# Attention's weights times values in plain fp32 with the turned weights stationary, and the sums of the second MLP product on VectorE

## The chip, the cores and the metric

One Trainium2 chip; the program uses one of its NeuronCores. A core has TensorE (PE, with its weight loads PEld), VectorE (DVE), ScalarE (ACT), GpSimd (POOL), and SyncE (SP), which here issues nearly all DMAs. The time is device microseconds of one execution, less is better; a kernel's time is the median of its runs. All tensors that enter and leave are float32.

## The reference, cut to what matters

One layer of an encoder on 1024 positions of width 1024, then a squared-ReLU MLP of width 4096. The first projection feeds four mixers; the change touches the attention mixer (4 heads, head width 64, two softmax maps of 32 channels each per head) and the second matrix product of the MLP.

```python
s = einsum('bqhmd,bkhmd->bhmqk', q_blk, k) * scale + bias     # m = 0, 1: two maps
p = softmax(s, axis=-1)
w = p[:, :, 0] - lam * p[:, :, 1]
o = einsum('bhqk,bkhe->bqhe', w, v)                            # weights times values
o = rmsnorm(o, subln_g) * (1.0 - lam_init)
...
x = x + concat(A, B, C, D) @ w_out
x = x + square(relu(rmsnorm(x) @ w_up)) @ w_down               # second product: @ w_down
x = rmsnorm(x)
```

## The kernel before, in words

**Order of work.** Everything is written out for one core. TensorE's instructions keep the order of the Python code. The other engines' order is set by a scheduler from the code, and each engine then works through its own queue in that order; the tile pools add waits between engines where a tile is written, read or reused. The stages follow one another: the mixers' projections and their own work (to about 240 us), attention (to about 500 us), the first MLP product (to 828 us), the second (to the end).

**fp32 products in three parts.** The kernel mostly multiplies with fp32r operands, in which TensorE takes a matrix at reduced precision. To keep fp32 accuracy a matrix is split in a high part (a cast on ScalarE) and a low part (source minus high part on VectorE, or on GpSimd where the code says so); `split` (lines 107 to 109) issues both, and `mm3` (115) multiplies high by high, high by low and low by high.

**Attention.** `attention` (738) walks over 16 units n, each one head and one pair of 128-row query blocks (i = 0, 1), in 4 slots kp. In each slot TensorE gets: scores of a block six slots ahead (`scores`, 621, into a `big` bank pair; VectorE takes the negated row maximum at line 657, ScalarE the exponential at 664, and `combine`, 669, subtracts the second map from the first without normalising, mostly on GpSimd); four 128x128 transposes of the weights (`turned`, 687); pieces of other work (`fill`: the output projection of the other three mixers); and for the slot before, weights times values (`apply`, 699). `turned` takes key blocks 2kp and 2kp+1 for both query blocks i, and splits the 128x512 result into a high and a low part in X12 or X13. The values lie in X4 or X5, split too, high part in columns 0 to 63 and low part in 64 to 127, so `apply` issues for each key block one product with all 128 columns stationary against the high weights (256 columns moving) and one with the 64 high columns against the low weights. The result is turned, with high and low contributions in different partitions; `heads_out` (715) adds and turns them back with two plain fp32 products with the constant `fold`. Then come the sum of squares (726), the reciprocal root, and `heads_scaled` (730), which writes the head's columns into `ya` on VectorE (line 735). From slot 43 on, `attended` and the functions of `w_out_a` read `ya`, and the residual and the second norm start.

**Second product.** `down` (1109) multiplies 2 halves of 4 hidden chunks by seven block products of a Strassen-like scheme, ORDER P1, P6, P2, P5, P7, P3, P4, four steps (pc = 0 to 3) each: 56 steps, 24 matmuls of 512 columns each. `prepare(s)` splits the two operands of step s (casts on ScalarE, subtracts on VectorE, line 109) into tile sets that alternate between even and odd steps, so a split waits until step s-2 has been multiplied; it also forms the sums of the `w_down` blocks that later products need, on GpSimd (lines 1067 to 1073), in place or into a new tile. `evict` (1094) adds a finished product's banks into `acc` on VectorE (1102); after P6 of the second half it also adds a common term to all of `acc`, on GpSimd (1105, 1107). For the last four steps `prepare` has two tile sets more, and the last three are prepared together after step 51, their operands in the three `stg` buffers.

Of the kernel before, what the change touches and what calls it, by code (L numbers as in the profile page):

```python
# [18 lines left out]
P = 128  # L19
S = 1024  # L20
D = 1024
NB = 8
# [22 lines left out]
class Trunk:  # L45
# [108 lines left out]
    def constants(self):  # L154
# [9 lines left out]
        self.fold = self.t("fold", [P, 64])  # L164
        nc.vector.tensor_copy(self.fold[0:64], self.ident[0:64, 0:64])
        nc.vector.tensor_copy(self.fold[64:128], self.ident[64:128, 64:128])
# [15 lines left out]
        self.vst = self.dr.tile([HEADS, P, NB, P], F32, name="vst", tag="vst")  # L182
# [429 lines left out]
    def load_v(self, h):  # L612
        v = self.t(f"X{4 + h % 2}", [P, NB, P], F32R)
        self.nc.sync.dma_start(v.bitcast(F32), self.vst[h])
        self.vs[h] = v
# [5 lines left out]
    def scores(self, n, step):  # L621
# [4 lines left out]
        if step == 0:  # L626
# [3 lines left out]
            else:  # L630
# [4 lines left out]
                if pr == 0:  # L635
                    self.load_v(h)
            self.st[n] = dict(h=h, pr=pr, sums=[None, None], rec=[None, None], w=[[None, None], [None, None]])
        st = self.st[n]
        qb = 2 * pr + i
        if m == 0:  # L640
            st["sums"][i] = self.small(2)
# [22 lines left out]
        nc.scalar.activation(p, sc, AF.Exp, bias=nm, accum_out=st["sums"][i][:, m:m + 1])  # L664
# [4 lines left out]
    def combine(self, n, i):  # L669
        nc = self.nc  # L670
        st = self.st[n]
        sums = st["sums"][i]
        rec = st["rec"][i] = self.small(2)
        nc.vector.reciprocal(rec, sums)
        cc = self.small(1)
        nc.vector.scalar_tensor_tensor(cc, sums[:, 0:1], self.neglam, rec[:, 1:2], op0=ALU.mult, op1=ALU.mult)
# [10 lines left out]
    def turned(self, n, kp):  # L687

        st = self.st[n]
        pv = self.sm().rearrange("p (k q) -> p k q", k=2)  # L690
# [6 lines left out]
        st["wt"] = st.get("wt", []) + [wt]  # L697

    def apply(self, n, kp):
        st = self.st[n]  # L700
        if kp == 0:
            st["av"] = self.sm("av")
        av, v, wt = st["av"], self.vs[st["h"]], st["wt"][kp]
        for kk in range(2):
            kb = 2 * kp + kk
# [3 lines left out]
            if kb == 0:  # L709
                self.mm(av[0:64, 0:256], v[:, kb, 0:64], wt[:, 1, kk, :], start=False, stop=False)  # L710
        if kp == 3:
            st["avs"] = self.t("avs", [P, 256], F32, bufs=2)
            self.nc.scalar.copy(st["avs"], av[:, 0:256])

    def heads_out(self, n):
        nc = self.nc
        st = self.st[n]
        po = self.sm()
        for i in range(2):
            self.mm(po[:, 64 * i:64 * i + 64], st["avs"][:, i * P:(i + 1) * P], self.fold, start=True, stop=True)  # L720
        ss = self.small(2)
        oo = self.t("oo", [P, P], F32, bufs=2)
        nc.scalar.copy(oo, po[:, 0:P])
        junk = self.t("junk", [P, P], F32)
        for i in range(2):
            nc.scalar.activation(junk[:, 64 * i:64 * i + 64], oo[:, 64 * i:64 * i + 64], AF.Square,
                                 scale=st["rec"][i][:, 0:1], accum_out=ss[:, i:i + 1])
        st["oo"], st["r"] = oo, self.rstd_of(ss, 64, 2)

    def heads_scaled(self, n):  # L730
        st = self.st.pop(n)
        h, pr = st["h"], st["pr"]
        for i in range(2):
            qb = 2 * pr + i
            self.nc.vector.tensor_scalar(self.ya[qb // 4][:, qb % 4, 64 * h:64 * h + 64], st["oo"][:, 64 * i:64 * i + 64],  # L735
                                         st["rec"][i][:, 0:1], st["r"][:, i:i + 1], op0=ALU.mult, op1=ALU.mult)
# [357 lines left out]
    def evict(self, half, name, r, bank):  # L1094
# [8 lines left out]
        if half == 1 and name == "P6":  # L1103
            tt = nc.gpsimd.tensor_tensor
# [4 lines left out]
    def down(self):  # L1109
# [18 lines left out]
        for s in range(0, n, 4):  # L1128
# [196 lines left out]
```

## Time and profile before

| | |
|---|---|
| time, median of 3 runs | 1174.46 us (1169.29 to 1174.57) |
| profiled execution, own time | 1172.41 us |
| its span in the trace | 1170.6 us |
| TensorE busy (share of span) | 1083.3 us (93%) |
| VectorE | 767.8 us (66%) |
| ScalarE | 529.6 us (45%) |
| GpSimd | 460.5 us (39%) |

The profiled execution lies between the runs timed. Busy times are sums of instruction spans; matmuls overlap, so TensorE's 93% is not 93% of its peak, and what a change is worth is read from the waits in its own stage.

### The profile page before, as it was taken

Reading aid. Unit: us, or ns where it says so; the run is one execution under the profiler, and the core shown is the slowest. Engines: PE = TensorE matmul, PEld = TensorE weight load, DVE = VectorE, ACT = ScalarE, POOL = GpSimd, SP = SyncE. Lnnn points to the kernel's source line nnn. Section 1 sums busy time; section 2 is a strip of 40 time slices with the busy share of each in tenths; the row PEclk is TensorE's granted clock in tenths of the full one; section 3 lists DMA queues with packets and bytes.
Section 4 is the critical chain, followed back from the end, with each engine's and each line's share of the span. In section 5 each row is a group of like instructions: output and inputs, shape, how many; then the busy total and the mean of one; then the engine's idle time right before and its main releaser. Section 6 shows DMA issues by size and latency. Waiting matters only on the chain.

```text
span 1170.6 us, 14927 instructions
## 1 busy us (share of the span) xinstructions
PE 1083.3 (93%) x5740; PEld 910.7 (78%) x5740; DVE 767.8 (66%) x914; ACT 529.6 (45%) x831; POOL 460.5 (39%) x304
## 2 busy tenths in 40 slices
PE   5999999979999876879999999999989999899987
PEld 4889887868988866767788888888767888678865
DVE  4459989678877778574443434344795556996673
ACT  5412213386677667453454545454433333323451
POOL 2000000244455545554746464645791002983001
PEclk9999999999999988998999999999999999999998
DMA  7113145971041121143444444446945552223223
GB/s 257 63 37 89 36 147 153 245 255 52 26 132 37 50 73 55 46 144 119 174 155 142 153 145 152 145 151 237 402 158 187 191 189 88 84 72 109 90 90 126
DMA packets 57284, 153.72 MB, mean 131 GB/s; under 512 B 6139, under 2 KB 11643, under 8 KB 57213
## 3 DMA queue, kind: packets, MB, share of 16 engines
q1 hardware_dynamic: 56205, 150.41, 38.3%
q0 software_dynamic: 1008, 2.36, 0.7%
q8 instruction: 45, 0.74, 0.3%
q14 instruction: 26, 0.21, 0.1%
HBM read 106.74 MB, written 47.19 MB: 131 GB/s over the span
## 4 chain that ended last, share of the span: by engine, by line
PE 73%; DVE 12%; ACT 6%; DMA 5%; issue 2%; POOL 1%; SPq 0%; POOLq 0%; ACTq 0%; DVEq 0%
PE big L102 35%; PE sm L102 29%; PE av L102 7%; DVE c L657 2%; PE sm L105 2%; DVE W L109 2%; DVE X L735 2%; DMA T<-in_w_down_dram 2%; DMA stg<-gd 1%; DVE X L109 1%; ACT X L108 1%; DVE T L212 1%; DVE T L109 1%; ACT W L664 1%; ACT W L108 1%
## 5 line engine op out<-in xcount | busy, mean ns | idle before, releaser
L109 DVE TENSOR_TENSOR W<-stg,W 128x1024 fp32r<-128x1024 f32 x82 | 137.1, 1673 | 140.3 <-ACT W L108 140.2
L108 ACT CAST W<-stg 128x1024 fp32r<-128x1024 f32 (+1 forms) x99 | 98.5, 997 | 282.3 <-PE big L102 184.4
L102 PE MATMUL big<-X,W 128*128 128x512 f32 x840 | 204.1, 397 | 0.5 <-DVE T L1005 0.5
L102 PEld LDWEIGHTS big<-X,W 128*128 128x128 f32 x840 | 157.7, 189 | 37.3 <-DVE T L1005 0.9
L102 PE MATMUL big<-T,W 128*128 128x512 f32 x696 | 170.2, 395 | 3.1 <-DVE T L109 2.3
L102 PEld LDWEIGHTS big<-T,W 128*128 128x128 f32 x696 | 130.1, 188 | 34.9 <-DVE T L109 3.6
L122 POOL TENSOR_TENSOR c<-c,mhalf 128x1 f32<-128x1 f32 (+3 forms) x46 | 33.6, 730 | 256.7 <-DVE c L126 222.3
L102 PE MATMUL sm<-W,X 128*128 128x256 f32 (+1 forms) x624 | 89.6, 294 | 0.8 <-DVE c L126 0.8
L657 DVE TENSOR_REDUCE c<-big 128x1 f32<-128x1024 f32 x64 | 77.9, 1219 | 16.4 <-PE big L102 15.7
L102 PE MATMUL big<-W,W 128*128 128x512 f32 x336 | 81.8, 399 | 4.6 <-DVE W L109 4.6
L102 PEld LDWEIGHTS sm<-W,X 128*128 128x128 f32 x624 | 79.4, 191 | 3.3 <-DVE c L126 1.0
L108 ACT CAST W<-T 128x1024 fp32r<-128x1024 f32 x48 | 50.4, 1049 | 68.5 <-PE big L102 61.6
L102 PE MATMUL sm<-W,T 128*128 128x256 f32 x576 | 78.6, 287 | 2.2 <-DVE T L133 1.4
L102 PEld LDWEIGHTS big<-W,W 128*128 128x128 f32 x336 | 64.0, 191 | 20.1 <-DVE W L109 5.9
L102 PE MATMUL sm<-W,W 128*128 128x512 f32 x260 | 71.0, 400 | 8.7 <-DVE W L109 4.1
L102 PE MATMUL sm<-T,W 128*128 128x512 f32 x286 | 77.2, 394 | 1.2 <-DVE T L109 1.2
L393 DVE SCALAR_TENSOR_TENSOR T<-T,vec,T 128x1024 f32<-128x1024 f32 x60 | 75.9, 1277 | 0.5
L109 DVE TENSOR_TENSOR W<-T,W 128x1024 fp32r<-128x1024 f32 x48 | 67.7, 1410 | 9.9 <-ACT W L108 9.2
L102 PEld LDWEIGHTS sm<-W,T 128*128 128x128 f32 x576 | 70.8, 189 | 2.9 <-DVE T L133 1.6
L102 PE MATMUL sm<-X,W 128*128 128x512 f32 x234 | 69.1, 406 | 0.4 <-DVE T L1005 0.4
L1067 POOL TENSOR_TENSOR T<-T,T 128x1024 f32<-128x1024 f32 x8 | 24.0, 3015 | 109.0 <-DVE T L109 107.9
L102 PEld LDWEIGHTS sm<-W,W 128*128 128x128 f32 x260 | 48.9, 190 | 22.2 <-DVE W L109 6.3
(256 smaller groups left out, 2046.5 us busy)
## 6 DMA issues: line engine op xcount, KB each, us to landing
stg<-gd SPq DMA_DIRECT2D x56, 512.0 KB, 3.3
gd<-T SPq DMA_DIRECT2D x32, 512.0 KB, 4.8
T<-in_w_down_dram SPq DMA_DIRECT2D x24, 512.0 KB, 4.7
stg<-in_w_up_dram SPq DMA_DIRECT2D x19, 512.0 KB, 4.4
T<-in_x_dram SPq DMA_DIRECT2D x16, 512.0 KB, 6.4
stg<-in_w_in_dram SPq DMA_DIRECT2D x16, 512.0 KB, 4.6
T<-in_w_up_dram SPq DMA_DIRECT2D x16, 512.0 KB, 4.2
gd<-X SPq DMA_DIRECT2D x16, 512.0 KB, 2.8
```

What stands on the lines that cost most here:

```text
L102: self.tc.keep_in_program_order(self.nc.tensor.matmul(*a, **k))
L105: self.tc.keep_in_program_order(self.nc.tensor.transpose(out, in_, self.ident))
L108: self.pin(self.nc.scalar.copy(hi, src))
L109: self.pin((eng or self.nc.vector).tensor_tensor(lo, src, hi.bitcast(F32), op=ALU.subtract))
L122: self.pin(self.nc.gpsimd.tensor_tensor(out, in_, self.mhalf[:, :w], op=ALU.pow))
L212: self.pin(nc.vector.scalar_tensor_tensor(xn, xt, r, gain, op0=ALU.mult, op1=ALU.mult))
L393: nc.vector.scalar_tensor_tensor(self.acc[c], z[:, j:j + S], self.dw_w[c][:, j:j + 1], self.acc[c], op0=ALU.mult, op1=ALU.add)
L657: nc.vector.tensor_reduce(nm, sc, axis=AX.X, op=ALU.max, negate=True)
L664: nc.scalar.activation(p, sc, AF.Exp, bias=nm, accum_out=st["sums"][i][:, m:m + 1])
L735: self.nc.vector.tensor_scalar(self.ya[qb // 4][:, qb % 4, 64 * h:64 * h + 64], st["oo"][:, 64 * i:64 * i + 64], st["rec"][i][:, 0:1], st[ ...
L1067: tt(t1, w["B12", pc], t1, op=ALU.subtract)
```

## The change

**Values and weights.** The values are stored unsplit (`v_cols`, `load_v`: two tiles that hold all heads, loaded once). `turned` transposes four key blocks of one query block and copies them unsplit, by ScalarE in even slots and by VectorE in odd ones. `apply` issues, for each key block, one plain fp32 product with the 128x128 turned weights stationary and 64 value columns moving; the result comes out with queries in the partitions, so `fold` and its products are gone. The normalising factor is put into the variance (two small VectorE instructions), and `heads_scaled` is one GpSimd instruction for both blocks (VectorE's for the last unit).

**Second product.** The sums of `prepare` and of `evict` move from GpSimd to VectorE. The first operands of the last four steps go to tiles X8 to X11, loaded at step 40; the last two steps are prepared after steps 48 and 49, into tiles that are free by then.

```diff
     def v_cols(self):
...
-            vv = self.t("avs", [P, HEADS, P], F32R, bufs=2)
-            src = pt.rearrange("p (h c) -> p h c", h=HEADS)
-            self.split(src, vv[:, :, 0:64], vv[:, :, 64:128])
-            nc.sync.dma_start(self.vst[:, :, tb, :].rearrange("h p x -> p h x"), vv.bitcast(F32))
+            vv = self.t("avs", [P, 256], bufs=2)
+            nc.scalar.copy(vv, pt)
+            nc.sync.dma_start(self.vst[tb // 4, :, tb % 4, :], vv)
...
     def turned(self, n, kp):
...
-        for i in range(2):
-            for kk in range(2):
-                kb = 2 * kp + kk
-                self.tr(pv[:, kk, i * P:(i + 1) * P], st["w"][i][0][:, kb * P:(kb + 1) * P])
-        wt = self.t(("X12", "X13")[kp % 2], [P, 2, 2, 256], F32R)
-        self.split(pv, wt[:, 0], wt[:, 1])
+        i, g = divmod(kp, 2)
+        pv = self.sm()
+        for x in range(4):
+            kb = 4 * g + x
+            self.tr(pv[:, x * P:(x + 1) * P], st["w"][i][0][:, kb * P:(kb + 1) * P])
+        if g == 0:
+            st["wt"][i] = self.t(f"X{12 + i}", [P, S])
+            self.nc.scalar.copy(st["wt"][i][:, 0:512], pv)
+        else:
+            self.nc.vector.tensor_copy(st["wt"][i][:, 512:], pv)
...
     def apply(self, n, kp):
...
-            if kb > 0:
-                self.mm(av[0:64, 0:256], v[:, kb, 0:64], wt[:, 1, kk, :], start=False, stop=False)
-            self.mm(av[:, 0:256], v[:, kb, :], wt[:, 0, kk, :], start=kb == 0, stop=kb == 7)
+            self.mm(av[:, 64 * i:64 * i + 64], wt[:, kb * P:(kb + 1) * P], self.vs[g][:, x, 64 * h:64 * h + 64],
+                    start=kb == 0, stop=kb == 7)
         if kp == 3:
-            st["avs"] = self.t("avs", [P, 256], F32, bufs=2)
-            self.nc.scalar.copy(st["avs"], av[:, 0:256])
+            st["oo"] = self.t("oo", [P, 2, 64], F32, bufs=2)
+            self.nc.scalar.copy(st["oo"], av[:, 0:P].rearrange("p (i c) -> p i c", i=2))
 
     def heads_out(self, n):
...
-        po = self.sm()
-        for i in range(2):
-            self.mm(po[:, 64 * i:64 * i + 64], st["avs"][:, i * P:(i + 1) * P], self.fold, start=True, stop=True)
...
+        s1 = st["sums"][:, :, 0]
+        nc.vector.scalar_tensor_tensor(v, s1, EPS, s1, op0=ALU.mult, op1=ALU.mult)
+        nc.vector.scalar_tensor_tensor(v, ss, 1.0 / 64, v, op0=ALU.mult, op1=ALU.add)
...
     def heads_scaled(self, n):
...
-            self.nc.vector.tensor_scalar(self.ya[qb // 4][:, qb % 4, 64 * h:64 * h + 64], st["oo"][:, 64 * i:64 * i + 64],
-                                         st["rec"][i][:, 0:1], st["r"][:, i:i + 1], op0=ALU.mult, op1=ALU.mult)
+        eng = self.nc.vector if n == 4 * HEADS - 1 else self.nc.gpsimd
+        eng.tensor_tensor(dst, st["oo"], st["r"].unsqueeze(2).broadcast_to([P, 2, 64]), op=ALU.mult)
...
     def load_g(self, s):
...
-        x = self.rg[s] = self.pair("stg")
+        last = s - len(self.steps) + 4
+        x = self.rg[s] = self.pair("stg" if last < 0 else f"X{8 + last}")
...
     def prepare(self, s):
...
-                (("T13", "T16"), ("T9", "T10")), (("T17", "T18"), ("T11", "T15")))
+                (("T13", "T16"), ("T5", "T6")), (("T17", "T18"), ("T7", "T8")))
...
-        if s + 3 < len(self.steps):
+        if s + 3 < len(self.steps) - 4:
             self.load_g(s + 3)
-        tt, w = self.nc.gpsimd.tensor_tensor, self.wq
+        tt, w = self.nc.vector.tensor_tensor, self.wq
...
     def evict(self, half, name, r, bank):
...
-            tt = nc.gpsimd.tensor_tensor
+            tt = nc.vector.tensor_tensor
...
     def down(self):
...
-                for y in (x + 2,) if x < n - 5 else range(x + 2, n):
-                    self.prepare(y)
+                if x == n - 16:
+                    for y in range(n - 4, n):
+                        self.load_g(y)
+                self.prepare(x + 2)
+                if n - 9 < x < n - 6:
+                    self.prepare(x + 6)
```

The order in which VectorE's queue stands, before and after, at three places. First, attention around one unit's `heads_scaled`; `c` are columns of 1 or 2 elements, `X` with `sm` the turned weights, `T` with `sm` the output projection's sums. Before:

```order
L657 TENSOR_REDUCE c_626_3591<-big_3586 128x1
L126 TENSOR_SCALAR c_617_3558<-c_614_3552 128x2
L109 TENSOR_TENSOR X_629_3600<-sm_3595,X_629_3600 128x512
L735 TENSOR_SCALAR X_315_2261<-oo_3553,c_513_3081,c_618_3560 128x64
L735 TENSOR_SCALAR X_315_2261<-oo_3553,c_529_3164,c_618_3560 128x64
L810 TENSOR_TENSOR T_401_2585<-sm_3605,T_401_2585 128x256
L657 TENSOR_REDUCE c_632_3634<-big_3629 128x1
L109 TENSOR_TENSOR X_637_3649<-sm_3644,X_637_3649 128x512
L674 RECIPROCAL c_634_3638<-c_624_3585 128x2
L676 SCALAR_TENSOR_TENSOR c_635_3640<-c_624_3585,neglam_922,c_634_3638 128x1
```

After:

```order
L650 TENSOR_REDUCE c_570_3414<-big_3409 128x1
L719 SCALAR_TENSOR_TENSOR c_582_3467<-c_581_3466,c_582_3467 128x2
L802 TENSOR_TENSOR T_379_2468<-sm_3389,T_379_2468 128x256
L650 TENSOR_REDUCE c_576_3450<-big_3445 128x1
L692 COPY X_573_3423<-sm_3460 128x512
L802 TENSOR_TENSOR T_387_2516<-sm_3435,T_387_2516 128x256
L667 RECIPROCAL c_578_3454<-c_548_3309 128x1
L669 SCALAR_TENSOR_TENSOR c_579_3456<-c_548_3309,neglam_919,c_578_3454 128x1
```

The two instructions of line 735 have left the queue, and each slot's subtract (L109) has become a copy (L692) in every second slot.

Second, steps 30 to 32 in the second product's second half, from the first subtract of step 30 on. A row with `stg` behind the arrow is the low part of a step's first operand, the other L109 row the low part of its `w_down` block. Before, with the sums in GpSimd's queue:

```order
L109 TENSOR_TENSOR W_1604_8804<-stg_8695,W_1603_8803 128x1024
L109 TENSOR_TENSOR T_1606_8808<-T_1508_8217,T_1605_8807 128x1024
L109 TENSOR_TENSOR W_1610_8841<-stg_8729,W_1609_8840 128x1024
L109 TENSOR_TENSOR W_1612_8845<-T_1515_8255,W_1611_8844 128x1024
L109 TENSOR_TENSOR W_1616_8878<-stg_8766,W_1615_8877 128x1024
L109 TENSOR_TENSOR T_1618_8882<-X_1592_8732,T_1617_8881 128x1024
```

After (L1060 and L1062 are the sums of P1, L1064 those of P6; T_1425 here is T_1508 above):

```order
L109 TENSOR_TENSOR W_1521_8597<-stg_8488,W_1520_8596 128x1024
L1060 TENSOR_TENSOR T_1414_7964<-T_1445_8122,T_1414_7964 128x1024
L109 TENSOR_TENSOR T_1523_8601<-T_1425_8010,T_1522_8600 128x1024
L1062 TENSOR_TENSOR X_1515_8562<-T_1471_8272,T_1414_7964 128x1024
L1064 TENSOR_TENSOR T_1445_8122<-T_1471_8272,T_1445_8122 128x1024
L1060 TENSOR_TENSOR T_1425_8010<-T_1453_8164,T_1425_8010 128x1024
L109 TENSOR_TENSOR W_1527_8634<-stg_8522,W_1526_8633 128x1024
L1062 TENSOR_TENSOR X_1525_8607<-T_1477_8312,T_1425_8010 128x1024
L1064 TENSOR_TENSOR T_1453_8164<-T_1477_8312,T_1453_8164 128x1024
L109 TENSOR_TENSOR W_1529_8638<-T_1432_8048,W_1528_8637 128x1024
L109 TENSOR_TENSOR W_1533_8671<-stg_8559,W_1532_8670 128x1024
```

Six sums now stand in the same queue, two of them between the two subtracts of step 31 (W_1527 and W_1529).

Third, from the last eviction of P3 on, when only P4's four steps are left. Before (step 53 is that of X_1598, W_1729 its first operand's low part; the T row with `stg` belongs to step 55):

```order
L1102 TENSOR_TENSOR T_1409_7690<-big_9224,T_1409_7690 128x512
L109 TENSOR_TENSOR T_1737_9652<-stg_9609,T_1736_9651 128x1024
L126 TENSOR_SCALAR c_1742_9663<-c_1741_9661 128x1
L109 TENSOR_TENSOR W_1729_9636<-stg_9541,W_1728_9635 128x1024
L212 SCALAR_TENSOR_TENSOR X_1740_9660<-T_1406_7687,c_1743_9665,gain_7703 128x1024
L109 TENSOR_TENSOR W_1731_9640<-X_1598_8769,W_1730_9639 128x1024
L126 TENSOR_SCALAR c_1746_9673<-c_1745_9671 128x1
```

After (step 53 is that of X_1587 and X_1515):

```order
L1095 TENSOR_TENSOR T_1326_7483<-big_9017,T_1326_7483 128x512
L126 TENSOR_SCALAR c_1659_9456<-c_1658_9454 128x1
L109 TENSOR_TENSOR W_1654_9445<-X_1587_9044,W_1653_9444 128x1024
L209 SCALAR_TENSOR_TENSOR X_1657_9453<-T_1323_7480,c_1660_9458,gain_7496 128x1024
L109 TENSOR_TENSOR W_1656_9449<-X_1515_8562,W_1655_9448 128x1024
L126 TENSOR_SCALAR c_1663_9466<-c_1662_9464 128x1
```

Step 53's two subtracts still stand behind the evictions, with a norm's instructions between them; those of steps 54 and 55 now stand further up.

## Rows read from the trace of the kernel before

**Rows 1.** windows: length, busy us (instructions) by engine, granted clock, DMA share, GB/s

```profile
400.00:450.00 50.00, 40.41 (x264) 35.41 (x263) 40.79 (x70) 36.86 (x77) 26.28 (x17) 0.93 0.17 60
450.00:500.00 50.00, 39.30 (x221) 33.03 (x220) 33.74 (x52) 28.17 (x60) 27.26 (x21) 0.90 0.13 49
```

**Rows 2.** 225 to 500 us by form: count, busy us, mean ns, idle before, releasers

```profile
L109 DVE TENSOR_TENSOR X<-sm,X 128x512 fp32r<-128x512 f32 x68 | 46.0, 682 | 6.7 <-ACT X L108 6.6
...
L735 DVE TENSOR_SCALAR X<-oo,c,c 128x64 f32<-128x64 f32 x32 | 24.9, 818 | 2.3 <-POOL c L122 2.3
...
L105 PEld LDWEIGHTS sm<-ident,X 128*128 128x128 f32 x192 | 23.4, 144 | 7.3 <-DVE X L735 4.3 <-issue 1.3
...
L102 PEld LDWEIGHTS av<-X,X 128*64 128x64 f32 x128 | 17.7, 140 | 17.6 <-DVE X L109 17.1
...
L102 PE MATMUL sm<-fold,avs 128*128 128x64 f32 x64 | 9.0, 263 | 0.5 <-ACT avs L713 0.5
L842 DVE TENSOR_TENSOR T<-sm,T 128x512 f32<-128x512 f32 x13 | 8.9, 687 | 5.8 <-PE sm L102 5.7
```

**Rows 3.** timeline of TensorE's weight loads in attention: start, us, instructions

```profile
341.03 0.53 PEld L102 LDWEIGHTS sm<-fold,avs 128*128 128x128 f32 x4
341.48 1.14 PEld L102 LDWEIGHTS sm<-W,T 128*128 128x128 f32 x9
...
346.18 0.54 PEld L102 LDWEIGHTS av<-X,X 128*64 128x64 f32 x4
346.64 0.19 PEld L102 LDWEIGHTS big<-X,X 112*128 112x128 f32 x1
```

**Rows 4.** line 735 by itself: shortest, median and longest ns

```profile
L735 DVE TENSOR_SCALAR X<-oo,c,c x32: 302/308/2360, 277.8 to 496.0; 128x64 f32<-128x64 f32 x32
```

**Rows 5.** chain that ended last, 345 to 351 us: start, us, what

```profile
346.32 2.35 DVE X L735 x2
...
350.13 0.61 DVE X L109
```

**Rows 6.** timeline, second product's first half: TensorE's first and tenth steps

```profile
827.57 5.72 PE L102 MATMUL big<-T,W 128*128 128x512 f32 x24
...
884.10 5.67 PE L102 MATMUL big<-W,W 128*128 128x512 f32 x24
```

**Rows 7.** timeline, second product, second half, 988 to 1068 us

```profile
988.01 2.66 DVE L1102 TENSOR_TENSOR X<-big,X 128x512 f32<-128x512 f32 x4 [0.92 <-PE big L102]
...
989.18 2.25 PE L102 MATMUL sm<-T,W 128*128 128x512 f32 x9
...
992.02 3.41 POOL L1071 TENSOR_TENSOR T<-T,T 128x1024 f32<-128x1024 f32 x1
993.09 3.42 DVE L109 TENSOR_TENSOR W<-T,W 128x1024 fp32r<-128x1024 f32 x1
...
1001.92 1.05 ACT L108 CAST W<-stg 128x1024 fp32r<-128x1024 f32 x1 [5.23 <-PE av L102]
...
1023.53 7.14 PE L102 MATMUL big<-W,W 128*128 128x512 f32 x23 [3.27 <-DVE W L109]
...
1065.80 5.72 PE L102 MATMUL big<-T,W 128*128 128x512 f32 x24
...
1067.18 1.21 DVE L109 TENSOR_TENSOR W<-stg,W 128x1024 fp32r<-128x1024 f32 x1
1068.32 1.21 DVE L109 TENSOR_TENSOR W<-T,W 128x1024 fp32r<-128x1024 f32 x1
```

**Rows 8.** timeline, last four steps

```profile
1132.17 1.56 PE L102 MATMUL sm<-T,W 128*128 128x512 f32 x6
...
1136.24 0.49 PE L102 MATMUL sm<-W,W 128*128 128x512 f32 x1 [2.50 <-ACT W L108]
...
1138.88 2.50 PE L102 MATMUL sm<-W,W 128*128 128x512 f32 x5 [2.15 <-DVE c L126]
...
1159.26 2.94 PE L102 MATMUL av<-T,T 128*128 128x512 f32 x12
```

More of the change, by code (lines that the diff above doesn't have):

```diff
@@ L163, in constants @@
         nc.vector.tensor_copy(self.identb, self.ident)
-        self.fold = self.t("fold", [P, 64])
-        nc.vector.tensor_copy(self.fold[0:64], self.ident[0:64, 0:64])
-        nc.vector.tensor_copy(self.fold[64:128], self.ident[64:128, 64:128])
         self.diag = self.t("diag", [P, HEADS, P], BF16)
@@ L610, in load_k, with load_v @@
             self.ks[h].append(kt)
[L612 to L615, printed above, removed]
+    def load_v(self):
+        self.vs = [self.t(f"X{4 + x}", [P, 4, 256]) for x in range(2)]
+        for x in range(2):
+            self.nc.sync.dma_start(self.vs[x], self.vst[x])
     def load_q(self, h, half, tag):
@@ L634, in scores @@
                     self.load_q(h, pr // 2, f"X{6 + h % 2}")
-                if pr == 0:
-                    self.load_v(h)
-            self.st[n] = dict(h=h, pr=pr, sums=[None, None], rec=[None, None], w=[[None, None], [None, None]])
+            self.st[n] = dict(h=h, pr=pr, sums=self.small(4).rearrange("p (i m) -> p i m", i=2),
+                              w=[[None, None], [None, None]], wt=[None, None])
         st = self.st[n]
         qb = 2 * pr + i
-        if m == 0:
-            st["sums"][i] = self.small(2)
         sc = self.big()
@@ L663, in scores @@
         p = self.t(tag, [P, S])
-        nc.scalar.activation(p, sc, AF.Exp, bias=nm, accum_out=st["sums"][i][:, m:m + 1])
+        nc.scalar.activation(p, sc, AF.Exp, bias=nm, accum_out=st["sums"][:, i, m:m + 1])
         st["w"][i][m] = p
@@ L671, in combine @@
         st = self.st[n]
-        sums = st["sums"][i]
-        rec = st["rec"][i] = self.small(2)
-        nc.vector.reciprocal(rec, sums)
+        sums = st["sums"][:, i, :]
+        rec = self.small(1)
+        nc.vector.reciprocal(rec, sums[:, 1:2])
         cc = self.small(1)
-        nc.vector.scalar_tensor_tensor(cc, sums[:, 0:1], self.neglam, rec[:, 1:2], op0=ALU.mult, op1=ALU.mult)
+        nc.vector.scalar_tensor_tensor(cc, sums[:, 0:1], self.neglam, rec, op0=ALU.mult, op1=ALU.mult)
         p1, p2 = st["w"][i]
@@ L689, in turned @@
         st = self.st[n]
-        pv = self.sm().rearrange("p (k q) -> p k q", k=2)
-        for i in range(2):
-            for kk in range(2):
-                kb = 2 * kp + kk
-                self.tr(pv[:, kk, i * P:(i + 1) * P], st["w"][i][0][:, kb * P:(kb + 1) * P])
-        wt = self.t(("X12", "X13")[kp % 2], [P, 2, 2, 256], F32R)
-        self.split(pv, wt[:, 0], wt[:, 1])
-        st["wt"] = st.get("wt", []) + [wt]
+        i, g = divmod(kp, 2)
[8 more added lines that the diff above has]
+            self.nc.vector.tensor_copy(st["wt"][i][:, 512:], pv)
     def apply(self, n, kp):
         st = self.st[n]
+        i, g = divmod(kp, 2)
         if kp == 0:
             st["av"] = self.sm("av")
-        av, v, wt = st["av"], self.vs[st["h"]], st["wt"][kp]
-        for kk in range(2):
-            kb = 2 * kp + kk
-            if kb > 0:
-                self.mm(av[0:64, 0:256], v[:, kb, 0:64], wt[:, 1, kk, :], start=False, stop=False)
-            self.mm(av[:, 0:256], v[:, kb, :], wt[:, 0, kk, :], start=kb == 0, stop=kb == 7)
-            if kb == 0:
-                self.mm(av[0:64, 0:256], v[:, kb, 0:64], wt[:, 1, kk, :], start=False, stop=False)
+        h, av, wt = st["h"], st["av"], st["wt"][i]
+        for x in range(4):
+            kb = 4 * g + x
+            self.mm(av[:, 64 * i:64 * i + 64], wt[:, kb * P:(kb + 1) * P], self.vs[g][:, x, 64 * h:64 * h + 64],
+                    start=kb == 0, stop=kb == 7)
         if kp == 3:
-            st["avs"] = self.t("avs", [P, 256], F32, bufs=2)
-            self.nc.scalar.copy(st["avs"], av[:, 0:256])
+            st["oo"] = self.t("oo", [P, 2, 64], F32, bufs=2)
+            self.nc.scalar.copy(st["oo"], av[:, 0:P].rearrange("p (i c) -> p i c", i=2))
     def heads_out(self, n):
@@ L717, in heads_out @@
         st = self.st[n]
-        po = self.sm()
-        for i in range(2):
-            self.mm(po[:, 64 * i:64 * i + 64], st["avs"][:, i * P:(i + 1) * P], self.fold, start=True, stop=True)
-        ss = self.small(2)
-        oo = self.t("oo", [P, P], F32, bufs=2)
-        nc.scalar.copy(oo, po[:, 0:P])
+        ss, v = self.small(2), self.small(2)
         junk = self.t("junk", [P, P], F32)
         for i in range(2):
-            nc.scalar.activation(junk[:, 64 * i:64 * i + 64], oo[:, 64 * i:64 * i + 64], AF.Square,
-                                 scale=st["rec"][i][:, 0:1], accum_out=ss[:, i:i + 1])
-        st["oo"], st["r"] = oo, self.rstd_of(ss, 64, 2)
+            nc.scalar.activation(junk[:, 64 * i:64 * i + 64], st["oo"][:, i, :], AF.Square, accum_out=ss[:, i:i + 1])
+        s1 = st["sums"][:, :, 0]
+        nc.vector.scalar_tensor_tensor(v, s1, EPS, s1, op0=ALU.mult, op1=ALU.mult)
+        nc.vector.scalar_tensor_tensor(v, ss, 1.0 / 64, v, op0=ALU.mult, op1=ALU.add)
+        st["r"] = self.small(2)
+        self.power(st["r"], v, 2)
     def heads_scaled(self, n):
         st = self.st.pop(n)
-        h, pr = st["h"], st["pr"]
-        for i in range(2):
-            qb = 2 * pr + i
-            self.nc.vector.tensor_scalar(self.ya[qb // 4][:, qb % 4, 64 * h:64 * h + 64], st["oo"][:, 64 * i:64 * i + 64],
-                                         st["rec"][i][:, 0:1], st["r"][:, i:i + 1], op0=ALU.mult, op1=ALU.mult)
+        h, qb = st["h"], 2 * st["pr"]
+        dst = self.ya[qb // 4][:, qb % 4:qb % 4 + 2, 64 * h:64 * h + 64]
+        eng = self.nc.vector if n == 4 * HEADS - 1 else self.nc.gpsimd
+        eng.tensor_tensor(dst, st["oo"], st["r"].unsqueeze(2).broadcast_to([P, 2, 64]), op=ALU.mult)
     def attention(self):
```

6 lines of the change are left out of this document (3 added, 3 removed).

## Prediction

> **What bounds the kernel now.** I read the page first: TensorE is busy for 93% of the span, so the question is where it waits. The windows show two stages with a problem. In attention's last third TensorE is busy for 40 of 50 us and its granted clock is 0.93 and 0.90 [rows 1], so for part of the time it is at the lower of its two levels. The groups by form say for whom it waits there: its weight loads for weights times values stand idle for 17.1 us behind the subtract of line 109, and the transposes for 4.3 us behind `heads_scaled`, line 735 [rows 2]. The chain shows why the subtract is late: 2.35 us of line 735 stand ahead of it on VectorE [rows 5]. By itself that instruction takes 0.31 us in the median, but up to 2.36 us [rows 4], when a GpSimd instruction is under way.
>
> The second product has a clean pace to compare with: from 1065.80 us to 1132.17 us it does twelve steps without a wait, 5.53 us each [rows 7, 8]. By that measure its first nine steps, 827.57 to 884.10 us, should take 49.8 us and take 56.5: 6.8 lost [rows 6]. Steps 28 to 39, 989.18 to 1065.80 us, take 76.6 instead of 66.4: 10.2 lost [rows 7]. The last four run from 1132.17 us to 1162.20 us, 30.0 instead of 22.1: 7.9 lost [rows 8]. Together 24.9 us. In the first two stretches the reason is in the durations: where GpSimd forms sums beside it, VectorE's subtract of 1024 columns takes 3.42 us and the sum 3.41; with GpSimd idle the same subtract takes 1.21 [rows 7]. TensorE then waits for the subtract, once for 3.27 us, after which 23 matmuls take 7.14 us where 24 take 5.72 [rows 7]. In the last stretch it waits twice, 2.50 and 2.15 us, for operands that are prepared only after step 51 [rows 8].
>
> **Attention: the products.** The trace of before holds the new instruction already: `fold`'s products are plain fp32 with 128x128 stationary and 64 columns moving, and the 32 of them show as 64 matmuls [rows 2], two weight loads and two matmuls each. Four loads take 341.03 to 341.48, 0.45 us, so a product costs 0.225 us [rows 3]. The old `apply` has four matmuls in a slot, 346.18 to 346.64, 0.46 us [rows 3]. The new one has four plain products, 0.90 us. Over 64 slots that adds 28.2 us; 16 times 0.45 us of `fold` go. TensorE gets **21.0 us** more to do.
>
> The Trainium skill ("FP8 and Floating Point Precision", TensorE Precision Notes) speaks against this change harder: true fp32 is four passes through the array. The trace does not agree, with two load and matmul pairs for one product; with four, the sum would be some 58 us higher, and that is the first rival below.
>
> **Attention: what goes.** Per unit VectorE loses four subtracts (0.682 us each) and two instructions of line 735 (0.818 each) and gains two copies of 128x512 out of PSUM [rows 2]. Before has no such copy; the nearest row is the two-operand add of that shape from PSUM, 0.687 us (line 842 [rows 2]), which I take; lower bounds than this only help. That is 3.0 us less in each unit. ScalarE loses two of four casts and a copy. One engine now does an eviction where two did it in turn. GpSimd gets 15 instructions of 128 columns, which nobody waits for except `attended`, three times; its wait stays about as long. So most of the wait behind line 109 should go: I take 13 of 17.1 us, 2 of the 4.3, and 2 us for a clock that falls less often. The bounds: nothing goes (0), or all 21.4 and all of the clock's loss, which is 0.07 and 0.10 of 50 us each [rows 1], 8.5 us together. Attention comes to 21.0 - 17 = **+4 us**, between -9 and +21. The vector work around `v_cols`, `combine` and the norm of the heads changes by small instructions beside TensorE's work: 0; without that cover it would be a few tenths per unit.
>
> **Second product: the sums.** A half has 16 sums, which P1 and P6 need formed in their eight steps or soon after. Two instructions of VectorE without GpSimd follow each other in 1.14 us, and an eviction takes 2.66/4 = 0.67 [rows 7]. Eight steps then hold 16 subtracts, 16 sums and up to 8 evictions, 36.5 + 5.3 = 41.8 us, in 44.2 us of TensorE's time. It fits, but with little room, and the order decides. The worst place is the one that the order of VectorE's queue shows: from the start of step 28, step 30's casts may start at 5.5 us, a cast takes 1.05 us [rows 7], its first subtract stands at 6.7, and the tenth instruction from there, step 31's second subtract, ends at 18.1; TensorE wants it at about 16.8: 1.3 us of waiting. In the same way I get 0.5 us before step 33, and 1 us behind P6's evictions, where VectorE now has 4 evictions, 4 adds of 512 and 4 of 1024 columns (10 us) in one stage. That is 3 us where 10.2 were lost: -7.2. In the first half ScalarE does P1's evictions, but the sums stand behind the transfers of `w_down` and ahead of the last evictions of the first product: 1.3 of 6.8 us left, -5.5. Bounds for both: no gain, and all 17.0.
>
> **Second product: the end.** Steps 54 and 55 are ready early. Step 53 is not: its tiles come free only with step 51's end, and behind that VectorE has an eviction, a first subtract, a pass of a norm and a second subtract. With casts of 1.05 and passes of 1.2 us [rows 7] the second ends some 4.7 us after step 51; TensorE wants it at 1.4. With 0.7 for the clock, 4 of 7.9 us are left: -3.9 (bounds 0 and -7.9). The four loads into X8 to X11 pass the others in SP's queue at step 40, ten steps before their use: 0.
>
> **Sum.** 1172.4 (the profiled execution, 2 us below the median of the runs) + 4 - 7.2 - 5.5 - 3.9 = 1159.8, **1160 us**.
>
> **Rivals.**
> *Plain products dearer than `fold` shows (slower).* If eight loads in a row do not overlap as four do, or a product had the four pairs of the rule, the slot's end grows. From 0.273 us a product on (0.225 + 12.4/256) the kernel is no faster than before; at 0.45 it is at 1217. For it: `fold`'s loads had other work behind them. Against it: 0.45 us for four is as long as the old `apply`'s four, which stand in a stream. Chance 0.05.
> *The waits in attention stay.* They are owed to the row maximum and the exponential as well, which don't change; then the 21 us stand nearly alone: 1172.4 + 18 - 16.6 = 1174, within 0.5%; with half of the relief 1166. For it: those stand in the same queues. Against: it is line 735 that the chain shows [rows 5]. Chance 0.13.
> *VectorE becomes the bound of the second product.* 95% of a stage leaves no room for the casts' lateness; if steps 29 to 39 lose 10 us again and the start 5, it is 1172.4 + 4 - 1.8 - 3.9 = 1171. Chance 0.10.
> *The new copy is held by GpSimd as line 735 is.* 32 copies with up to 2 us each eat what line 735 gives back: about 1170. The Trainium skill ("Advanced Engine Details and Errata", VectorE Performance Modes) asks source and destination in SBUF for the mode that shares GpSimd's port, so by it a copy from PSUM is not held; no run here shows it. Chance 0.04.
> *Attention gains too.* All waits and most of the slow clock go: 1172.4 - 5 - 17 = 1150. Chance 0.13.
>
> **How the numbers follow.** The forecast, 1153 to 1167 us, has 0.55; the rivals 0.45. 0.5% is about what a measurement of this kernel can tell from no change, 5.9 us of 1174.5; faster means below 1168.6. That holds for the forecast, for attention's gain, and for half of the waits' rival and a third of VectorE's and the copy's: 0.55 + 0.13 + 0.07 + 0.05 = 0.80. Slower than 1180.3 are the dear products and a little of the rest, 0.06; between lie 0.14. The range is 1147 to 1171: below it lies a tenth of attention's gain, above it the dear products and the worse half of the waits' rival.
>
> **What the profile of the changed kernel would show.** Products: 512 matmuls of `av`, 0.11 us apart. Attention: the idle time of `av`'s loads behind VectorE below 5 us, no VectorE instruction of the heads above 1 us, the clock above 0.93 from 400 to 500 us. Second product: subtracts of 1.2 us throughout, no GpSimd beside them, steps 28 to 39 in about 69 us, the last four in about 26. It would be wrong if `av`'s loads stood further apart than 0.14 us, if TensorE's waits in attention only changed their releaser, or if subtracts in the second product stood in VectorE's queue for longer than a step.

## The result and the profile after

| | before | changed |
|---|---|---|
| median (lowest to highest), us | 1174.51 (1169.29 to 1174.90), 4 runs | 1159.56 (1158.61 to 1163.62), 4 runs |
| ratio, 95% interval | | 0.9889 [0.9853, 0.9926] |
| profiled execution, its own time / span, us | 1172.41 / 1170.6 | 1158.61 / 1156.8 |

The kernel is 1.1% faster, 0.4 us from the forecast. One of all the executions reported here, the profiled one of e10, was slow (1358.31 us at a granted clock of 0.75), and nothing is compared with it. On the page of the changed kernel, the line of busy times shows TensorE busy for more of the span (93% before), and the chain that ended last shows less of VectorE (12% before):

```profile
PE 1097.3 (95%) x5932; PEld 932.0 (81%) x5932; DVE 729.8 (63%) x897; ACT 505.5 (44%) x783; POOL 346.0 (30%) x279
...
PE 82%; DVE 7%; ACT 3%; DMA 3%; issue 3%; POOL 1%; SPq 1%; POOLq 0%; ACTq 0%; DVEq 0%
```

**Where the gain lies.** The second product's first step starts at 827.99 us; before it started at 827.57 [rows 6]. In these two profiles attention and all that precedes the second product thus take the same time, and from that mark to the end of the span it is 328.8 us instead of 343.0.

**Attention.** First the groups by form from 225 to 500 us, as in [rows 2] (TensorE's weight loads, then VectorE):

```profile
L102 PEld LDWEIGHTS av<-X,X 128*128 128x128 f32 x512 | 64.0, 197 | 5.7 <-DVE X L692 4.9
L105 PEld LDWEIGHTS sm<-ident,X 128*128 128x128 f32 x192 | 23.3, 146 | 3.8 <-DVE X L728 2.3
...
L692 DVE COPY X<-sm 128x512 f32<-128x512 f32 x32 | 21.7, 679 | 1.6 <-PE sm L105 1.6
L719 DVE SCALAR_TENSOR_TENSOR c<-c,c 128x2 f32<-128x2 f32 x16 | 20.7, 1292 | 1.2 <-ACT junk L716 1.2
L718 DVE SCALAR_TENSOR_TENSOR c<-c 128x2 f32<-128x2 f32 x16 | 6.6, 415 | 0.0
```

256 products are 512 loads, two for each, and their idle time behind VectorE has fallen from 17.1 to 4.9 us. But line 719, an instruction of two columns that is new, takes 1.29 us in the mean. The timelines of its engine and of GpSimd show what stands beside it:

```profile
341.55 1.90 DVE L719 SCALAR_TENSOR_TENSOR c<-c,c 128x2 f32<-128x2 f32 x1
...
341.01 2.42 POOL L678 TENSOR_TENSOR X<-X,W 128x1024 f32<-128x1024 f32 x1
```

It ends at 343.45 us, within 0.02 of the GpSimd addition beside it; the shortest of the 16, with no GpSimd instruction beside it, takes 0.14 us. The price of a product is read from the timeline of weight loads, and the windows show what became of the stage's clock (columns as in [rows 1]):

```profile
344.73 0.98 PEld L102 LDWEIGHTS av<-X,X 128*128 128x128 f32 x8
345.63 0.19 PEld L102 LDWEIGHTS big<-X,X 112*128 112x128 f32 x1
```

```profile
400.00:450.00 50.00, 44.26 (x312) 40.96 (x312) 40.64 (x61) 31.55 (x64) 27.91 (x22) 0.93 0.16 56
450.00:500.00 50.00, 42.67 (x254) 37.38 (x253) 31.20 (x45) 24.80 (x52) 28.06 (x23) 0.90 0.15 55
```

Eight loads take 344.73 to 345.63, 0.90 us for four products, as forecast. TensorE is busier than in [rows 1], by 3.9 and 3.4 us, but the clock is the same, 0.93 and 0.90.

**Second product.** Its places in the timeline that answer to [rows 6 to 8], VectorE's row first:

```profile
988.75 1.21 DVE L109 TENSOR_TENSOR W<-stg,W 128x1024 fp32r<-128x1024 f32 x1
...
827.99 5.72 PE L102 MATMUL big<-T,W 128*128 128x512 f32 x24
...
879.92 5.67 PE L102 MATMUL big<-W,W 128*128 128x512 f32 x24
...
985.00 2.25 PE L102 MATMUL sm<-T,W 128*128 128x512 f32 x9
...
1038.30 2.12 PE L102 MATMUL sm<-W,W 128*128 128x512 f32 x8 [1.15 <-DVE W L109]
...
1055.00 5.71 PE L102 MATMUL big<-T,W 128*128 128x512 f32 x24
...
1121.38 1.55 PE L102 MATMUL sm<-T,W 128*128 128x512 f32 x6
1124.02 0.50 PE L102 MATMUL sm<-W,W 128*128 128x512 f32 x1 [1.08 <-ACT W L108]
1126.66 1.84 PE L102 MATMUL sm<-W,W 128*128 128x512 f32 x5 [2.14 <-DVE W L109]
1128.30 4.13 PE L102 MATMUL sm<-T,T 128*128 128x512 f32 x12
...
1146.18 2.94 PE L102 MATMUL av<-T,T 128*128 128x512 f32 x12
```

| stretch | lost before, us | lost after, us | forecast left, us |
|---|---|---|---|
| steps 0 to 8 | 6.8 | 879.92 - 827.99 - 49.8 = 2.1 | 1.3 |
| steps 28 to 39 | 10.2 | 1055.00 - 985.00 - 66.4 = 3.6 | 3 |
| the last four | 7.9 | 1149.12 - 1121.38 - 22.1 = 5.6 | 4 |

The subtract takes 1.21 us where it took 3.42, and the longest wait in steps 28 to 39 is 1.15 us where it was 3.27. In the last four, both waits are there still; behind the second, 12 matmuls take 4.13 us where 12 take 2.94.

### The profile page after: what moved, and what is told of

The parts are those of the page before. It is cut to its first block, busy times and chain, and to the rows that moved or that the text cites. A ratio compares the mean times of both kernels' runs of the same rounds, so it can differ in the third digit from the quotient of the medians.

```text
span 1156.8 us, 15172 instructions
## 1 busy us (share of the span) xinstructions
PE 1097.3 (95%) x5932; PEld 932.0 (81%) x5932; DVE 729.8 (63%) x897; ACT 505.5 (44%) x783; POOL 346.0 (30%) x279
## 4 chain that ended last, share of the span: by engine, by line
PE 82%; DVE 7%; ACT 3%; DMA 3%; issue 3%; POOL 1%; SPq 1%; POOLq 0%; ACTq 0%; DVEq 0%
PE big L102 37%; PE sm L102 32%; PE av L102 10%; PE sm L105 3%; DVE W L109 2%; DVE T L209 1%; DMA vst<-avs 1%; DVE c L650 1%; ACT T L207 1%; ACT W L108 1%; DVE T L109 1%; DMA gain<-in_norm_g_dram 1%; ACT W L657 1%; DMA stg<-in_w_out_dram 0%; ACT X L108 0%
## 5 line engine op out<-in xcount | busy, mean ns | idle before, releaser
L109 DVE TENSOR_TENSOR W<-stg,W 128x1024 fp32r<-128x1024 f32 x80 | 103.6, 1296 | 140.6 <-ACT W L108 140.5
L102 PEld LDWEIGHTS big<-W,W 128*128 128x128 f32 x336 | 62.9, 188 | 15.2 <-DVE W L109 1.3
L102 PE MATMUL av<-X,X 128*128 128x64 f32 x512 | 64.9, 275 | 4.5 <-DVE X L692 4.5
L102 PEld LDWEIGHTS av<-X,X 128*128 128x128 f32 x512 | 64.0, 197 | 5.7 <-DVE X L692 4.9
L109 DVE TENSOR_TENSOR W<-T,W 128x1024 fp32r<-128x1024 f32 x48 | 59.6, 1241 | 9.9 <-ACT W L108 9.0
```

The source lines that it names most:

```text
L102: self.tc.keep_in_program_order(self.nc.tensor.matmul(*a, **k))
L109: self.pin((eng or self.nc.vector).tensor_tensor(lo, src, hi.bitcast(F32), op=ALU.subtract))
```

## The experiments

### Which half of the change gives the gain

Two kernels take one half of the change each, whole; two more are the kernel of before with one edit of the second product (e4 with the change's tiles for the last four as well). In the diffs, `...` marks lines left out.

e3:

```diff
-        tt, w = self.nc.gpsimd.tensor_tensor, self.wq
+        tt, w = self.nc.vector.tensor_tensor, self.wq
...
-            tt = nc.gpsimd.tensor_tensor
+            tt = nc.vector.tensor_tensor
```

e4:

```diff
-        x = self.rg[s] = self.pair("stg")
+        x = self.rg[s] = self.pair("stg" if last < 0 else f"X{8 + last}")
...
-                for y in (x + 2,) if x < n - 5 else range(x + 2, n):
-                    self.prepare(y)
+                if x == n - 16:
+                    for y in range(n - 4, n):
+                        self.load_g(y)
+                self.prepare(x + 2)
+                if n - 9 < x < n - 6:
+                    self.prepare(x + 6)
```

> Only the attention of the change, with the second MLP product as it was before (its sums on GpSimd, its last four steps' operands in the old places). Theory: the waits that go (17 us) are paid by dearer products on TensorE (+21 us) and the stage comes out level: the time is 1174 to 1178 us, and the second product starts within 1 us of where it started before (827.6 us). Rival 1 (attention gains, its waits were worth more than its products): 1165 us or less. Rival 2 (products dearer than the fold showed, and the second product hides it in the sum): 1180 us or more.

> Only the second product of the change (sums on VectorE, last four steps' operands prepared early), with the attention as it was before. Theory: the whole gain is here, 1160 to 1163 us (13 to 14 us under before). Rival (the gain needs the new attention as well, or attention gave part of it): 1167 us or more.

> Before with one edit: the sums of weight blocks in the second product on VectorE instead of GpSimd; the preparation of the last four steps stays where it was. Theory: steps 0 to 8 lose 2 us instead of 6.8, steps 28 to 39 lose 3.6 instead of 10.2, and the last four stay at 7.9: 1162 to 1164 us. Rival (VectorE was already late there and the sums only move the wait): 1172 us or more.

> Before with one edit: the operands of the last four steps loaded and split earlier, in other tiles, the sums still on GpSimd. Theory: only the end gains, 7.9 us lost becomes 5.6: 1171 to 1173 us. Rival 1 (the end's loss is the clock and not the waits): 1174 us, no change. Rival 2 (without GpSimd's sums out of the way the earlier splits come late too): 1175 us or more.

All four ran on one chip, where before took 1174.57 us. "To the mark" is the start of the second product's first step in the profile, "from it" the rest of the span. For before and for the changed kernel these two columns come from the profiles shown above, and the changed kernel's time is the one above: it was not timed again beside the experiments, so "over" and "below the changed kernel" compare separate measurements here and later.

| kernel | median, us | ratio [95%] | to the mark | from it |
|---|---|---|---|---|
| before | 1174.57 | | 827.57 | 343.0 |
| e1, attention alone | 1173.23 | 0.9989 [0.9976, 1.0001] | 829.96 | 341.6 |
| e2, second product alone | 1160.09 | 0.9884 [0.9859, 0.9909] | 827.21 | 330.4 |
| e3, sums alone | 1164.02 | 0.9913 [0.9883, 0.9942] | 832.97 | 331.3 |
| e4, end alone | 1171.98 | 0.9978 [0.9962, 0.9993] | 831.18 | 340.2 |
| changed (as above) | 1159.56 | 0.9889 [0.9853, 0.9926] | 827.99 | 328.8 |

The gain is the second product's: 14.5 us with it alone, 1.3 with attention alone, an interval that reaches no change. e1 misses its range by 0.8 us, and its mark, expected within 1 us of 827.6, stands at 829.96; e2, e3 and e4 came in their ranges, e3 at the upper end. Sums (10.6) and end (2.6) together give 13.1 of the 14.5. One caution for reading a single profile: before, e2, e3 and e4 run the same code up to the mark and reach it between 827.2 and 833.0 us, while kernels with the changed second product take 328.8 to 330.9 from it. The 0.4 us by which the two profiles' attentions differ mean no more than "level".

### What a plain product costs on the path

```diff
+            for y in range(2):
                 self.mm(av[:, 64 * i:64 * i + 64], wt[:, kb * P:(kb + 1) * P], self.vs[g][:, x, 64 * h:64 * h + 64],
-                    start=kb == 0, stop=kb == 7)
+                        start=kb + y == 0, stop=kb + y == 8)
```

> The changed kernel with each of the 256 plain products of weights times values issued twice into the same sum (the sum is twice as large, which the norm behind it takes out again, up to its small constant). It measures what one plain product costs on the path. Theory: 0.22 us each and TensorE sets the pace, +52 to +57 us on the changed kernel's 1159.6, 1211 to 1217 us. Rival (the products lie partly in time in which TensorE waits anyway): under 1200 us. Rival (a product costs more than the fold showed, some of it hidden until now): over 1225 us.

Measured: 1198.15 us, ratio 1.0200 [1.0180, 1.0221], 38.6 us over the changed kernel. The first rival's bound (under 1200) is the one that holds. TensorE's group by form from 225 to 560 us and the windows of this kernel:

```profile
L102 PE MATMUL av<-X,X 128*128 128x64 f32 x1024 | 119.5, 272 | 0.0
```

```profile
400.00:450.00 50.00, 50.00 (x429) 48.90 (x428) 24.03 (x44) 23.08 (x48) 23.04 (x17) 1.00 0.10 30
450.00:500.00 50.00, 48.64 (x372) 45.13 (x370) 41.09 (x56) 31.54 (x64) 26.59 (x21) 1.00 0.21 75
```

The same group in the changed kernel:

```profile
L102 PE MATMUL av<-X,X 128*128 128x64 f32 x512 | 64.9, 275 | 4.5 <-DVE X L692 4.5
```

256 more products make TensorE busy for 54.6 us more, 0.213 each, near the 0.225 of the forecast. The time grows by 16 us less. TensorE's waits (all groups of the waits' view added) fall from 26.0 us, from 228 to 560 us in the changed kernel, to 15.2 us, from 228 to 600 us in this one, which comes to the same work some 40 us later: part of the added work stands where it waited. The other 5 us fit the clock, 1.00 from 400 to 500 us where the changed kernel has 0.93 and 0.90. So a term for products and a term for waits are not independent here.

### Why the waits in attention went

Both kernels put 64 VectorE instructions of the old subtract's length back. In the first the products wait for them, in the second for ScalarE's copy alone.

Both:

```diff
-            self.nc.scalar.copy(st["wt"][i][:, 0:512], pv)
-        else:
-            self.nc.vector.tensor_copy(st["wt"][i][:, 512:], pv)
+        w = st["wt"][i][:, 512 * g:512 * g + 512]
+        self.nc.scalar.copy(w, pv)
```

e6:

```diff
+        self.nc.vector.tensor_tensor(w, pv, w, op=ALU.max)
```

e7:

```diff
+        self.nc.vector.tensor_tensor(pv, pv, w, op=ALU.max)
```

> The changed kernel with the order of work of the old split put back, without its cheaper products: each turned half is copied by ScalarE first and then passed through VectorE (the larger of two equal numbers, 64 instructions of the length of the old subtracts), and the products wait for VectorE. Theory: the waits of before were this chain of two engines, so some 10 to 17 us of idle come back in the attention: 1169 to 1177 us. Rival (the waits went because the heads' scaling left VectorE, not because the chain is shorter): 1163 us or less.

> The same VectorE instructions as in the run with the chain put back, but their output goes back to PSUM and the products wait for ScalarE's copy alone; only the bank is free later. Theory: VectorE has the time (its busy share there is about 70%), so the load without the chain costs little: within 4 us of the changed kernel, 1158 to 1164 us. Rival (VectorE's load is what made the products late, not the chain): within 3 us of the run with the chain, 1168 us or more.

Measured: e6 1172.99 us, ratio 0.9986 [0.9972, 1.0001]; e7 1168.05 us, 0.9956 [0.9939, 0.9973]. The windows of e6, of e7 and of the changed kernel at the end of attention:

```profile
425.00:525.00 100.00, 89.41 (x493) 78.67 (x492) 68.88 (x104) 57.55 (x117) 48.99 (x40) 0.83 0.18 62
```

```profile
425.00:525.00 100.00, 84.98 (x504) 74.85 (x504) 71.91 (x107) 56.34 (x116) 52.94 (x43) 0.90 0.21 74
```

```profile
425.00:525.00 100.00, 82.57 (x499) 72.53 (x499) 70.56 (x103) 56.46 (x114) 57.22 (x45) 0.91 0.24 83
```

e6's time is the one expected, but not by the way expected: its waits from 228 to 560 us come to 29.1 us, only 3.1 more than in the changed kernel, not 10 to 17, and its products wait behind line 692 for 2.5 us, less than the changed kernel's 4.5. What is lower is the clock in this profile, 0.83 instead of 0.91, some 8 of the 100 us. e7, expected within 4 us, costs 8.5, which is the time of its rival, though 4.9 us from e6. The lists of waits from 228 to 425 us name a new one, in e6 and in e7:

```profile
PE sm L105 <- DVE X L692: 4.6, 9, 0.7
```

```profile
PE sm L105 <- DVE sm L692: 4.8, 9, 0.8
```

TensorE's transposes wait for the PSUM bank that VectorE still reads. So more than half of e6's 13.4 us comes with the instructions themselves and the longer-held bank, without the chain of two engines. The other 4.9 us do not show in the waits, which are 29.8 us in e7, 0.7 more than in e6; the clock differs, but one profile each can't settle it.

Before, the waits were 43.7 us. With the chain and its instructions back they are 29.1, so most of the 17.7 us that went did not go because the chain was shortened, nor, as far as e8 below shows, because the scaling of the heads left VectorE. What is left is that TensorE's longer products stand in the time in which it waited before, as the doubled ones do. That is inferred from what the other runs leave over; no run isolates it.

### The old stall and the new one

e8:

```diff
-        eng = self.nc.vector if n == 4 * HEADS - 1 else self.nc.gpsimd
-        eng.tensor_tensor(dst, st["oo"], st["r"].unsqueeze(2).broadcast_to([P, 2, 64]), op=ALU.mult)
+        for i in range(2):
+            self.nc.vector.tensor_scalar(dst[:, i], st["oo"][:, i], st["r"][:, i:i + 1], None, op0=ALU.mult)
```

e9:

```diff
...
+        nc.scalar.activation(st["oo"][:, :, 64], st["sums"][:, :, 0], AF.Copy, scale=math.sqrt(64 * EPS))
-            nc.scalar.activation(junk[:, 64 * i:64 * i + 64], st["oo"][:, i, :], AF.Square, accum_out=ss[:, i:i + 1])
-        nc.vector.scalar_tensor_tensor(v, s1, EPS, s1, op0=ALU.mult, op1=ALU.mult)
-        nc.vector.scalar_tensor_tensor(v, ss, 1.0 / 64, v, op0=ALU.mult, op1=ALU.add)
+            nc.scalar.activation(junk[:, i, :], st["oo"][:, i, :], AF.Square, accum_out=ss[:, i:i + 1])
...
```

> The changed kernel with the scaling of the heads on VectorE for all units, as two instructions of the old form each, instead of one on GpSimd. Theory: they are held by GpSimd now and then as before (0.82 us in the mean) and each held one makes a copy behind it late; 2 to 4 us of waits come back: 1160 to 1164 us. Rival (this was the main cause of the waits of before): 1168 us or more. Rival (the held instruction is only exchanged for the small one of the new norm, so nothing changes): within 1 us of 1159.6.

> The changed kernel without the two small VectorE instructions of the new norm: the square of the sum of the weights goes into the square's own accumulation as a 65th column (one small ScalarE copy), and the factor 8 into the scale of the heads. It takes 20.7 us of held time off VectorE. Theory: in 300 to 400 us nothing waits for it, and late in the attention the norm that stands behind is then held itself by the same GpSimd additions, so little is won: 1157 to 1160 us, within 2.5 us of the changed kernel. Rival (the held small instructions cause the waits that are left at 425 to 500 us): 1154 us or less.

e8: 1159.30 us, ratio 0.9870 [0.9855, 0.9885], no difference from 1159.56; the second rival's time, not the 1160 to 1164 of the theory. Its line by itself:

```profile
L728 DVE TENSOR_SCALAR X<-oo,c x32: 236/246/1361, 276.2 to 495.5; 128x64 f32<-128x64 f32 x32
```

It is held rarely (0.28 us in the mean against 0.82 in [rows 2]), so the run shows that these instructions cost nothing on VectorE, but not what the old holds cost. For that the changed kernel itself speaks: line 719 takes 20.7 us in all, 18.4 more than 16 of its shortest would, where line 735's 24.9 were 15.2 more than 32 of its shortest, and in the window from 300 to 400 us TensorE is busy for all of the 100 us.

e9: 1156.65 us, ratio 0.9815 [0.9773, 0.9858], 2.9 us below the changed kernel's median, just past the expectation's edge; before took 1175.54 us on that chip, up to 1180.73, so part of the better ratio may be due to that. In its profile the mark stands at 827.13 us, 0.9 us earlier, and the waits behind the norm (line 209) are 4.7 us instead of 5.9. The held small instructions are not what causes most of the waits that are left.

### Two edits further

e10:

```diff
-        if i == 1 and n >= 5:
+        if i == 1 and 5 <= n < 12:
```

e11:

```diff
-                (("T13", "T16"), ("T5", "T6")), (("T17", "T18"), ("T7", "T8")))
-        at, bt = sets[last if last >= 0 else s % 2]
+                (("T13", "T16"), ("T5", "T6")), (("T17", "T18"), ("T7", "T8")), (("W0", "W1"), ("X2", "T0")))
+        at, bt = sets[4 if last == 1 else last if last >= 0 else s % 2]
...
-                self.prepare(x + 2)
+                if x + 2 != n - 3:
+                    self.prepare(x + 2)
+                if x == n - 9:
+                    self.prepare(n - 3)
```

In e11 the last norms' outputs go to other tiles, too. e12 has the edits of e9, e10 and e11.

> The changed kernel with the second block's combination of the two maps on VectorE (one instruction of 1.59 us) for the last four units instead of ScalarE and a GpSimd addition of 2.4 us, which hold the norms there (3.3 us instead of 1.27). Theory: two of the waits at 425 to 470 us go or shrink by 2 to 5 us with a part of the half clock behind them, against 6 us more on VectorE: 1154 to 1159 us. Rival (VectorE is the late engine there, whoever holds it, as in the run with more load on it): 1161 us or more.

> The changed kernel with the operands of the second of the last four steps split three steps earlier into tiles of their own. Theory: the two waits at the start of the last four steps (1.1 and 2.1 us) and the half clock behind them (about 1.8 us) go, 27.7 us become 22.5 to 23.5: 1154 to 1156 us. Rival (the final norms of the first four blocks, queued on the same engines, make the next thing late): 1158 us or more.

> The three last edits together: no small held instructions, the second block's combination on VectorE for the last four units, and the second of the last four steps prepared early. Theory: the end's 5 us are independent of the attention; of the attention's two edits, each worth 2 to 3 us at most, the one takes from VectorE about what the other gives to it: 1150 to 1154 us. Rival (the attention's two edits lose their gains together, the clock's half-speed spells staying): 1155 us or more.

e10: 1157.66 us, 0.9831 [0.9791, 0.9871], in the expected range; that the two waits shrank as argued isn't shown. e11: 1155.01 us, 0.9810 [0.9775, 0.9844], as expected. Its last four steps in the timeline:

```profile
1122.68 1.56 PE L102 MATMUL sm<-T,W 128*128 128x512 f32 x6
1124.08 0.39 PE L102 MATMUL sm<-X,W 128*128 128x512 f32 x1
...
1142.15 2.93 PE L102 MATMUL av<-T,T 128*128 128x512 f32 x12
```

1122.68 to 1145.08 us, 22.4 where the changed kernel takes 27.7, and no wait: the late operand of one step was all of the loss at the end, clock included. e12: 1147.59 us (1144.64 to 1149.98), ratio 0.9762 [0.9734, 0.9791], 2.4 us below the lowest expected and clear of the changed kernel's interval. Whether the attention's two edits take from each other stays open: by the medians e9, e10 and e11 gain 2.9, 1.9 and 4.6 us, 9.4 together, and e12 12.0, but by the ratios the three gain 2.1% of before together, and e12 1.3%. In e12's profile (1149.98 us, the slowest of its runs) the mark stands at 824.70 us, 3.3 earlier, and from it to the end it takes 323.5 us, the same as e11. Of TensorE's waits from 425 to 560 us that are left in it, three rows:

```profile
PE sm L105 <- DVE T L209: 5.8, 2, 3.0
PE av L105 <- DVE X L109: 5.1, 3, 2.5
...
PE av L102 <- DVE X L692: 0.6, 1, 0.6
```

The wait of the products behind the copy, 4.3 us in the changed kernel, has gone to 0.6; the norms' wait has not.

## Why the prediction was right, step by step

**Sum.** 1160 against 1159.56, but by two misses that cancel: attention was forecast at +4 and came out level (+0.4 in the profile, -1.3 alone), and the second product at -16.6 and came to -14.5 alone, -14.2 in the profile. By the profiles the two parts are off by 3.6 and 2.4 us in opposite directions; that the sum is met to 0.4 us is luck.

**Products, +21.0.** Right in kind: two pairs of load and matmul (x512 for 256 products), 0.225 us by the loads and 0.213 by TensorE's busy time. With 0.213 the term is 64 x (0.853 - 0.46) - 7.2 = 18.0. The rival of dearer products falls with it, at 0.45 us a product as at 0.273. The prediction also took the two pairs to speak against the Trainium skill's four passes through the array ("FP8 and Floating Point Precision", TensorE Precision Notes). That was read too far: how many passes lie within a pair, no record here shows.

**Waits and clock, -17.** TensorE's waits from 228 to 560 us add up to 43.7 us before and 26.0 after, 17.7 less, which with the 18.0 gives the level. The two waits named went nearly as forecast, 17.1 to 4.9 us and 4.3 to 2.3; the clock, of which 2 us were hoped for, gave nothing (0.93 and 0.90, as in [rows 1]), and other waits went in its place. The reason given, less work on VectorE and one engine where two took turns, failed for the most part: with both put back, e6's waits are 3.1 us longer and not 17. The prediction added the products and the waits as if the one left the other alone, and e5 shows that they are not independent. And that line 735 was the culprit the chain of waits named is not borne out: line 719 is held for as much in all, with TensorE busy throughout beside it from 300 to 400 us.

**Small instructions, 0.** The forecast that no VectorE instruction of the heads would be above 1 us was wrong. It had drawn on the rule on performance modes only. The copy from PSUM indeed isn't held (0.673 to 0.693 us, all 32), and that rival falls. The Trainium skill has a second rule ("GPSIMD Engine Reference", Specifications): the ports are contended for, too, by a VectorE instruction with two inputs in SBUF. Line 719 has them, and its row agrees (0.14 us at the shortest, 1.29 in the mean); without the two small instructions the kernel is 2.9 us faster by the medians (e9).

**Sums, -7.2 and -5.5.** -6.6 and -4.7 measured. The queue was read rightly: subtracts at 1.21 us, a wait of 1.15 us behind P6's evictions where 1 was forecast, 0.60 and 0.34 before steps 31 and 33 where 1.3 and 0.5 were. VectorE did not become the bound. In the first half the wait is 1.08 us (at 840.53 us), and the 0.8 us more than forecast are slower matmuls soon behind it: a step of 5.88 us for 5.53 from 845.96 us, and nine matmuls in 2.50 for 2.09 from 851.84. The granted clock is 1.00 there; what slows them isn't shown.

**End, -3.9.** -2.3 measured: the term that was mis-sized most in proportion. The waits, 3.2 us together, agree with the 4.7 - 1.4 forecast, but behind them come 1.2 us in the 12 slow matmuls and 0.5 in the five before, where 0.7 for the clock was taken. e11 confirms the cause: with step 53's operands ready, waits and slow matmuls go together.

## What to carry to other kernels

Plain fp32 products with 64 moving columns cost about twice the split ones' TensorE time here (0.90 us a slot for 0.46), and the waits that went paid for no more than that. Do not add the price of new work and the waits it relieves as if they were independent: work added on TensorE fills time in which it waited. Moving the sums from GpSimd to VectorE gave 10.6 us although VectorE got 40 instructions more (e3), because its subtracts with two SBUF inputs take 1.21 us without a GpSimd sum beside them, and 3.42 with one. When a wait is shortened by preparing operands early, follow each operand of each step: one left in its old tile kept 5 of the 8 us (e11).

## What the runs showed of the hardware

A VectorE instruction of 128x2 on two SBUF operands takes 0.14 us, or up to 2.11 beside a GpSimd addition of 128x1024 that began before it, and ends with that addition (343.45 and 343.43 us); its size says nothing about its price. With added work on TensorE the clock fell less: with every product doubled the granted clock from 400 to 500 us was 1.00 in place of 0.93 and 0.90, which with part of the waits filled made 54.6 us of added work cost 38.6.
